# Stick-breaking attention: meta columns of four blocks turned in one transpose, first tokens' values added behind PSUM, 528 scores as 256 and 272

## The chip, the cores and the metric

The kernel runs on one core of a Trainium2 chip. The metric is the device time of one execution in microseconds, as the median of several runs. A core has five engines with a queue each, which run their instructions in order and wait for each other through semaphores: TensorE (PE in the profile; its weight loads are PEld), VectorE (DVE), ScalarE (ACT), GpSimd (POOL) and SyncE (SP), which issues the DMAs here. Tiles lie in SBUF; matmuls write to PSUM, which has eight banks of 128 x 512 float32.

## The reference

A decoder layer with two attention branches on the same normalized input: 16 meta tokens, then 2048 tokens, model width 1024. One branch is stick-breaking attention with 8 heads of 64:

```python
def stick_breaking_attention(q, k, v, valid):
    ...
    for blk in range(L // BLOCK):
        q0 = blk * BLOCK
        end = q0 + BLOCK
        z = jnp.einsum('bqhd,bkhd->bhqk', q[:, q0:end], k[:, :end],
                       preferred_element_type=jnp.float32) * scale
        ...
        mask = (s[None, :] < t[:, None]) & valid[None, :end]
        log_beta = jax.nn.log_sigmoid(z)
        log_1m = jnp.where(mask, log_beta - z, 0.0)
        rev = lax.cumsum(log_1m, axis=3, reverse=True)
        suffix = jnp.concatenate([rev[..., 1:], jnp.zeros_like(rev[..., :1])], axis=-1)
        w = jnp.where(mask, jnp.exp(log_beta + suffix), 0.0)
        outs.append(jnp.einsum('bhqk,bkhd->bqhd', w.astype(v.dtype), v[:, :end]))
    return jnp.concatenate(outs, axis=1)
```

The weight of a key is the product of `1 - sigmoid` over the keys between it and the query, times its own sigmoid. So with `r` the running product of `sigmoid(-z)` from the query backwards, the weights are differences of neighbours in `r`, and the sum over keys can be written as `r` times differences of neighbouring values, plus the value of the first token behind the query. The kernel computes it in that form. The other branch is a sliding-window attention with sinks; gates, two branch projections, an output projection and norms surround both.

## The kernel before

Tokens run in reverse order in four groups of 512 (`g`), in two halves: groups 2 and 3 first, then 1 and 0. Precision is kept by splitting each float32 operand into a high and a low part (`h`, `l`), so that most products are three matmuls. Each half has three stages. The first computes the projections for both branches and, woven between them, the sliding-window attention (`attend`). In the second, `stick` is woven into the gate projections (`tiles_by_tile`, `gemm`, L454) by `weave`, which hands out steps of `stick` by a credit that `cost_sb` sets. The third is other gate work (half 0) or the output (half 1).

The order of TensorE's instructions is written by hand over the whole kernel (`manual_schedule`); those of the other engines and the DMA queue are, for most stages, put in order by a scheduler. SP issues almost all DMAs.

`stick` runs over units: one head `h` (8) and one query group `g` (4), 32 units. In a unit, `row(h, g, n, j)` computes the scores of query block `j` (128 queries) against the next four key blocks: two matmuls per bank (L916), a sigmoid out of PSUM by ScalarE into `r` (L920), and a running product by DVE (`tensor_tensor_scan`, L928 or L930). The last row of a block (`end`) also has the 16 meta columns. For `j` = 0 it has 512 + 16 = 528 columns, more than a bank holds: `own` rows put the 16 into a second bank `zm` with two more matmuls (L918) and one more activation (L922). The others end with 400, 272 and 144 columns.

`turn`, `lt` steps later (6 in half 0, 5 in half 1), transposes blocks of rows with up to four transposes into a bank `t` (L941) and evicts them split into high and low (`evac_split`, L119 by ScalarE, L120 by DVE). At the end of a unit `turn_meta` transposes the meta columns of the four blocks, four transposes of 16 columns each into `zm` (L952), and evicts them split into rows 0 to 15 and 32 to 47 of `wm` (one of two 128x512 tiles).

`values` (L967) takes the turned tiles two steps later and accumulates weights times value differences in bank `o`, of which there is one. The unit's last matmul there takes `wm` against `vm[:, p, a]`, 128 rows: the meta differences in rows 0 to 15 and 32 to 47, and in rows from 64 the first tokens' values of the blocks, picked by constants in `wm` from row 64 on, which are set by a memset and an `affine_select` (L859, L860) at the start of each `stick`. Then `o` is copied out by ScalarE (L971) and stored. The next unit's first matmul into `o` waits for that copy.

`sb_v` in the projection stages makes the value differences. Its `firsts` (called by `late`) takes the first token's values of eight blocks, gathered in `vf`, transposes them (L578), splits them and writes them to `vm` by a DMA; there are eight such calls. `meta` makes the meta differences and `turned` puts them into `vm` (L594 and after), once for each of four pairs of heads, in half 0; L596 copies them to rows 32 to 47.

POOL does the splitting of weights in half 0's stick stage (L115, L116) and the causal masking of rows in half 1's (`affine_select`, L925).

Of the kernel before, what the change touches and what calls it, by code (L numbers as in the profile page):

```python
# [16 lines left out]
P = 128  # L17
# [31 lines left out]
def tile_kernel(ctx, tc, x, xt, meta, metat, gain, w_in, w_sb, w_sw, w_out, sinks, fgain,  # L49
# [23 lines left out]
    vn = cp.tile([P, 4], F32, name="vn")  # L73
    vf = cp.tile([P, 16], F32, name="vf")
    cp.tile([P, 40], F32, name="pad")
    ident = cp.tile([P, P], F32, name="ident")
# [11 lines left out]
    for i in range(IDLE):  # L88
        T.matmul(idle[:, :8 * 48], lhsT=mx.rearrange("p k t -> p (k t)")[:, :P], rhs=mx.rearrange("p k t -> p (k t)"), start=True, stop=True)
    V.memset(f32(vm), 0.0)  # L90

# [456 lines left out]
    def sb_v(p):  # L548

        def use(g, acc, ms):  # L550
            t, d = tmp(), tmp()
            A.copy(t, acc)
            V.tensor_tensor(d[:, :GT - 1], t[:, 1:], acc[:, :GT - 1], op=ALU.subtract)
            f0 = p % 2 * 8
            A.copy(vf[:, f0 + g % 2 * 4:f0 + g % 2 * 4 + 4], t.rearrange("p (b q) -> p b q", b=4)[:, :, 0])

# [17 lines left out]

            def firsts():

                tr = ps("zm")
                T.transpose(tr[:8, :P], vf[:, f0:f0 + 8], ident)  # L578
                vb = tmp(F32R)[:8, :2 * P].rearrange("p (a d) -> p a d", a=2)
                meta_rows(tr[:8, :P], vb[:, :, 0:64], vb[:, :, 64:128])  # L580
                DMA(vm[64 + 4 * g:72 + 4 * g, p], vb)

            def meta():
# [8 lines left out]
                def turned():  # L592
                    tr = ps("t")
                    T.transpose(tr[:NM, :P], md, ident)  # L594
                    meta_rows(tr[:NM, :P], vm[0:NM, p, :, 0:64], vm[0:NM, p, :, 64:128])
                    A.copy(vm[32:32 + NM, p], f32(vm[0:NM, p]))  # L596
                    rows()
                soon.append(turned)

            if ms is None:  # L600
                join(vn[:, p:p + 1] if g % 2 else vf[:, f0 + 4:f0 + 5])
            pending.append(rows if ms is None else meta)
            if g % 2 == 0:
                pending.append(lambda: late.append(firsts))
        return weights(C_SBV + p * P), use, "back"
# [242 lines left out]
    def stick(groups, bp):  # L848
# [4 lines left out]
        for tag, shape, n in (("q1", [P, GT], 2), ("q2", [P, GT], 2), ("v", [P, 4, P], 5), ("wh", [P, GT], 3), ("wl", [P, GT], 3),  # L853
                              ("k", [P, KW], 2)):
            for _ in range(n):
                bp.tile(shape, F32R, tag=tag, name=tag, bufs=n)
        for g in groups:
            w = wm[g % 2]
            G.memset(f32(w), 1.0)  # L859
            G.affine_select(out=w, in_=f32(w), pattern=[[-1, 4], [0, P]], compare_op=ALU.is_equal, fill=0.0,  # L860
                            base=-64 - 4 * g, channel_multiplier=1)
        av_todo = []
# [36 lines left out]
        def row(h, g, n, j):  # L899
# [10 lines left out]
            k0 = (b0 - 4 * groups[0]) * P  # L910
            own = end and nb == 4
            z = ps("z")
            zm = ps("zm") if own else None
            for t, qt in enumerate(st["q"]):
                lq = qt[:, j * P:(j + 1) * P]
                T.matmul(z[:, :w], lhsT=lq, rhs=kt[h][:, k0:k0 + w], start=t == 0, stop=t == 1)  # L916
# [3 lines left out]
            A.activation(r[:, :w], z[:, :w], AF.Sigmoid, scale=-1.0)  # L920
            if own:
                A.activation(r[:, w:w + NM], zm[:, :NM], AF.Sigmoid, scale=-1.0)  # L922
                w += NM
            if n == 0 and mask is None:
# [6 lines left out]
            last[j] = r[:, w - 1:w]  # L931
            rows_of[h, g, n, j] = r

        def turn(h, g, n, i):
# [13 lines left out]
        def turn_meta(h, g):  # L948
            p, a = divmod(h, 2)
            tr = ps("zm")  # L950
            for j in range(4):
                T.transpose(tr[:NM, j * P:(j + 1) * P], rows_of[h, g, 3 - g, j][:, GT - P * j:GT - P * j + NM], ident)  # L952
            w = wm[g % 2]
            evac_split(w[0:NM], w[32:32 + NM], tr[:NM])
            av_todo.append((h, g, vm[:, p, a, :], w, None, False, True))

        def values():
# [10 lines left out]
            if last:  # L968
                p, a = divmod(h, 2)
                u = tmp()  # L970
                A.copy(u, o)  # L971
                for n in range(2):
                    DMA(od[p][g][n][64 * a:64 * a + 64], u[64 * n:64 * n + 64])
# [5 lines left out]
        for s in range(n + lt + 3):  # L979
# [4 lines left out]
            if 0 <= t < n:  # L984
# [336 lines left out]
    for half, groups in enumerate(halves):  # L1321
# [61 lines left out]
        with tc.tile_pool(name=f"sb{half}", bufs=1, side="left") as bp:  # L1383
# [106 lines left out]
```

## Time and profile before

| | us |
|---|---|
| median of three runs | 2112.88 (2112.0 to 2113.49) |
| the profiled execution | 2112.16 |
| its span, first to last instruction | 2110.4 |
| stick-breaking of half 0 within it | about 374 to 592 |
| stick-breaking of half 1 within it | about 1092 to 1612 |

The profile is one execution. Busy time is given for each engine; matmuls are pipelined, so that the duration of one is longer than the distance to the next, and TensorE's cost of a piece of work is read from start to start. A row of a group reads: line, engine, operation, out<-in, partitions x elements, count | busy us, mean ns of one | idle time of the engine before them, and what ended it. A row of a timeline reads: start, length, engine, line, operation, tiles, count. A row of waits reads: who waited for whom, us in total, times, longest. What two matmuls in a row do in the same bank is merged into one row (x2).

### The profile page before, as it was taken

The numbers are of one execution on the slowest core, as the hardware profiler recorded it, in microseconds if no ns is written. First come the engines' busy times: TensorE is split into PE (matmuls) and PEld (weight loads), VectorE is DVE, ScalarE is ACT, GpSimd is POOL, SyncE is SP. The second block draws the span as 40 slices with busy tenths as digits, with TensorE's granted clock in tenths as the row PEclk, the third lists the DMA queues.
The fourth block names the chain that finished last, engine by engine and source line by source line (L and its number), as shares of the span: only waits on it lengthen the run. The fifth ranks groups of instructions, "written<-read, shape, count | busy, mean of one in ns | idle before, by whom it ended". The sixth has DMA issues, their size and how long they took to land.

```text
span 2110.4 us, 30845 instructions
## 1 busy us (share of the span) xinstructions
PE 2094.4 (99%) x10695; PEld 1755.2 (83%) x10695; DVE 1479.1 (70%) x2375; ACT 1058.8 (50%) x2438; POOL 300.1 (14%) x484
## 2 busy tenths in 40 slices
PE   9999999999999999999999999999999999999998
PEld 7888888888878888888888888888888888788887
DVE  7897986888878554887738888877774456564553
ACT  6677774555646335777735555555553202221131
POOL 2133444211000000232310000000000232000000
PEclk9999999999999999999999999999999999999999
DMA  9955545766449674435455344343424996568532
GB/s 337 324 174 193 191 168 181 238 194 200 139 142 338 232 256 155 152 136 178 137 172 153 123 126 127 118 125 95 123 88 142 360 323 203 181 232 309 160 100 90
DMA packets 169580, 391.07 MB, mean 185 GB/s; under 512 B 23601, under 2 KB 27697, under 8 KB 169425
## 3 DMA queue, kind: packets, MB, share of 16 engines
q1 hardware_dynamic: 169136, 388.84, 54.9%
q8 instruction: 85, 1.39, 0.3%
q14 instruction: 71, 0.57, 0.1%
q10 hardware_dynamic: 288, 0.27, 0.0%
HBM read 241.68 MB, written 145.18 MB: 183 GB/s over the span
## 4 chain that ended last, share of the span: by engine, by line
PE 91%; DVE 3%; ACT 3%; DMA 2%; issue 1%; SPq 0%; ACTq 0%; DVEq 0%
PE ps_g L454 39%; PE ps_o L967 6%; PE ps_z L916 6%; PE ps_t L941 6%; PE ps_z L754 3%; PE ps_o L810 2%; PE ps_g L252 1%; PE ps_g L253 1%; PE ps_g L251 1%; PE ps_z L252 1%; PE ps_z L251 1%; PE ps_z L253 1%; PE ps_t L252 1%; PE ps_t L253 1%; PE ps_t L251 1%; PE ps_t L788 1%
## 5 line engine op out<-in xcount | busy, mean ns | idle before, releaser
L454 PE MATMUL ps_g<-xh,wh 128*128 128x512 f32 x1296 | 532.1, 411 | 0.8 <-DVE tmp L675 0.5
L454 PE MATMUL ps_g<-xl,wh 128*128 128x512 f32 x1296 | 507.6, 392 | 0.4 <-DVE xl L1169 0.3
L454 PE MATMUL ps_g<-xh,wl 128*128 128x512 f32 x1296 | 507.7, 392 | 0.0
L930 DVE TENSOR_TENSOR_SCAN row<-row 128x512 f32<-128x512 f32 (+4 forms) x256 | 297.1, 1161 | 91.9 <-ACT row L920 39.5
L454 PEld LDWEIGHTS ps_g<-xh,wl 128*128 128x128 f32 x1296 | 243.3, 188 | 54.4 <-DVE wl L1217 0.4
L920 ACT ACTIVATE row<-ps_z 128x512 f32<-128x512 f32 (+1 forms) x320 | 172.4, 539 | 213.5 <-PE ps_z L916 192.3
L454 PEld LDWEIGHTS ps_g<-xh,wh 128*128 128x128 f32 x1296 | 244.3, 188 | 41.4 <-ACT xh L1168 1.0
L454 PEld LDWEIGHTS ps_g<-xl,wh 128*128 128x128 f32 x1296 | 244.8, 189 | 37.8 <-DVE xl L1169 1.7
L119 ACT ACTIVATE wth<-ps_t 128x512 fp32r<-128x512 f32 (+1 forms) x320 | 170.7, 533 | 76.3 <-PE ps_t L941 75.2
L120 DVE SCALAR_TENSOR_TENSOR wtl<-ps_t,wth 128x512 fp32r<-128x512 f32 (+1 forms) x320 | 188.9, 590 | 25.3 <-ACT wth L119 24.8
L916 PE MATMUL ps_z<-kt,q 128*128 128x512 f32 (+3 forms) x640 | 185.3, 369 | 0.0
L941 PE MATMUL ps_t<-ident,row 128*128 128x128 f32 x1088 | 171.7, 273 | 0.1
L941 PEld LDWEIGHTS ps_t<-ident,row 128*128 128x128 f32 x1088 | 134.7, 140 | 34.0 <-DVE wtl L120 1.3
L916 PEld LDWEIGHTS ps_z<-kt,q 128*128 128x128 f32 x640 | 117.9, 188 | 23.5
L967 PE MATMUL ps_o<-wth,vc 128*128 128x512 f32 (+1 forms) x320 | 130.2, 407 | 0.0
L967 PE MATMUL ps_o<-wtl,vc 128*128 128x512 f32 (+1 forms) x320 | 116.3, 363 | 0.0
L762 ACT ACTIVATE sc<-sc,nm 128x129 f32<-128x129 f32 x256 | 100.0, 393 | 27.9 <-DVE nm L760 26.9
L115 POOL TENSOR_SCALAR wh<-raw 128x1024 fp32r<-128x1024 f32 (+1 forms) x47 | 52.8, 1124 | 354.0 <-PE ps_g L454 143.4
L610 ACT ACTIVATE tmp<-ps_g 128x512 f32<-128x512 f32 x84 | 50.3, 598 | 74.1 <-PE ps_g L454 67.0
L925 POOL TENSOR_SCALAR_AFFINE_SELECT row<-row 128x128 f32<-128x128 f32 x64 | 20.4, 318 | 468.2 <-ACT row L920 441.0
L290 ACT CAST ringl<-gt 128x512 fp32r<-128x512 f32 x32 | 19.9, 622 | 129.0 <-DVE gt L288 127.1
L794 POOL TENSOR_SCALAR_AFFINE_SELECT pm<-pl 64x256 fp32r<-64x256 f32 x128 | 74.3, 580 | 37.3 <-DVE pl L120 31.9
(441 smaller groups left out, 4130.1 us busy)
## 6 DMA issues: line engine op xcount, KB each, us to landing
wh<-h_in_w_in SPq DMA_DIRECT2D x66, 512.0 KB, 3.7
wl<-l_in_w_in SPq DMA_DIRECT2D x66, 512.0 KB, 4.9
h_in_w_in<-wh SPq DMA_DIRECT2D x50, 512.0 KB, 3.3
l_in_w_in<-wl SPq DMA_DIRECT2D x50, 512.0 KB, 3.5
raw<-in_w_in SPq DMA_DIRECT2D x49, 512.0 KB, 5.3
q<-qd SPq DMA_DIRECT2D x128, 128.0 KB, 3.3
vc<-vd SPq DMA_DIRECT2D x48, 256.0 KB, 3.1
kd<-tmp SPq DMA_DIRECT2D x32, 256.0 KB, 3.3
```

The costliest lines, as they stand in the source:

```text
L119: A.activation(h, acc, AF.Copy, scale=scale)
L120: V.scalar_tensor_tensor(l, acc, scale, f32(h), op0=ALU.mult, op1=ALU.subtract)
L251: T.matmul(acc, lhsT=wh[:, k, :], rhs=h, start=k == 0, stop=False)
L252: T.matmul(acc, lhsT=wh[:, k, :], rhs=l, start=False, stop=False)
L454: T.matmul(acc, lhsT=a[:, k, :], rhs=b[:, k, :], start=k == i == 0, stop=k == KT - 1 and i == 2)
L762: A.activation(sc[:, hh, :], sc[:, hh, :], AF.Exp, bias=nm[:, hh:hh + 1], accum_out=den[:, hh:hh + 1])
L794: G.affine_select(out=pm[to, :, c], in_=full[r, :, c], pattern=[[0, 4], [sign, HB]], compare_op=ALU.is_ge, fill=0.0, base=n - 1, channel_m ...
L916: T.matmul(z[:, :w], lhsT=lq, rhs=kt[h][:, k0:k0 + w], start=t == 0, stop=t == 1)
L920: A.activation(r[:, :w], z[:, :w], AF.Sigmoid, scale=-1.0)
L930: V.tensor_tensor_scan(r[:, :w], r[:, :w], r[:, :w], last[j] if n else 1.0, op0=ALU.mult, op1=ALU.min)
L941: T.transpose(tr[:, j * P:(j + 1) * P], rows_of[h, g, n - (j > i), j][:, k0:k0 + P], ident)
L967: T.matmul(o[:, :n], lhsT=v, rhs=r, start=first and r is wh, stop=last)
```

## The change

- `turn_meta`: the 16 meta columns of an end row are copied by POOL into a tile `m` of the unit, split into high and low (two operations for each end row, four end rows a unit). One transpose turns the 128 columns of `m` (4 blocks x 2 parts x 16) at once; four copies, two by ScalarE and two by DVE, put the 32 rows of each block beside its own 128 columns of `wm`, which is zero elsewhere (block-diagonal). The `wm` are set to zero once at the start, and their constants go.
- `vm` holds the meta differences in all 128 rows, eight times; three DMAs from SBUF to SBUF double them, each from what the one before wrote.
- First tokens: `firsts` goes. `vf` keeps the first values by column; POOL copies them into `vfirst`, which has a head's values in its half of the partitions and zeros in the other. `values` adds them as it evicts `o`: four activations of 128 columns with a bias for each partition, in place of one copy of 512.
- Own rows: 528 scores are 256 in a bank `z` and 272 in `zm`, two matmuls and one sigmoid each.
- The step costs handed to `weave` for `turn_meta` become 0.11 for 0.43, and `cost_sb` follows. `dynamic_dma_scratch_size=1024` and a wider `pad` move what lies where in SBUF.

```diff
-    vf = cp.tile([P, 16], F32, name="vf")
-    cp.tile([P, 40], F32, name="pad")
+    vf = cp.tile([P, 4, 8], F32, name="vf")
+    vfirst = [cp.tile([P, 4, 8], F32, name=f"vf{a}") for a in range(2)]
+    cp.tile([P, 88], F32, name="pad")
...
-    V.memset(f32(vm), 0.0)
+    for t in (*(f32(w) for w in wm), *vfirst):
+        G.memset(t, 0.0)
...
-            def firsts():
-
-                tr = ps("zm")
-                T.transpose(tr[:8, :P], vf[:, f0:f0 + 8], ident)
-                vb = tmp(F32R)[:8, :2 * P].rearrange("p (a d) -> p a d", a=2)
-                meta_rows(tr[:8, :P], vb[:, :, 0:64], vb[:, :, 64:128])
-                DMA(vm[64 + 4 * g:72 + 4 * g, p], vb)
...
-                    A.copy(vm[32:32 + NM, p], f32(vm[0:NM, p]))
+                    for n in (NM, 2 * NM, 4 * NM):
+                        DMA(vm[n:2 * n, p], vm[0:n, p])
...
             if g % 2 == 0:
-                pending.append(lambda: late.append(firsts))
+                for a, t in enumerate(vfirst):
+                    r = slice(64 * a, 64 * a + 64)
+                    G.tensor_copy(t[r, p], vf[r, p])
...
-        for g in groups:
-            w = wm[g % 2]
-            G.memset(f32(w), 1.0)
-            G.affine_select(out=w, in_=f32(w), pattern=[[-1, 4], [0, P]], compare_op=ALU.is_equal, fill=0.0,
-                            base=-64 - 4 * g, channel_multiplier=1)
...
-            own = end and nb == 4
-            z = ps("z")
-            zm = ps("zm") if own else None
+            pieces = [("z", 0, w)]
+            if end and nb == 4:
+                pieces = [("z", 0, w // 2), ("zm", w // 2, w // 2 + NM)]
+                w += NM
+            banks = [ps(tag) for tag, _, _ in pieces]
             for t, qt in enumerate(st["q"]):
-                lq = qt[:, j * P:(j + 1) * P]
-                T.matmul(z[:, :w], lhsT=lq, rhs=kt[h][:, k0:k0 + w], start=t == 0, stop=t == 1)
-                if own:
-                    T.matmul(zm[:, :NM], lhsT=lq, rhs=kt[h][:, k0 + w:k0 + w + NM], start=t == 0, stop=t == 1)
+                for z, (_, c, m) in zip(banks, pieces):
+                    T.matmul(z[:, :m], lhsT=qt[:, j * P:(j + 1) * P], rhs=kt[h][:, k0 + c:k0 + c + m], start=t == 0, stop=t == 1)
             r = bp.tile([P, RW], F32, tag="row", name="row", bufs=12)
-            A.activation(r[:, :w], z[:, :w], AF.Sigmoid, scale=-1.0)
-            if own:
-                A.activation(r[:, w:w + NM], zm[:, :NM], AF.Sigmoid, scale=-1.0)
-                w += NM
+            for z, (_, c, m) in zip(banks, pieces):
+                A.activation(r[:, c:c + m], z[:, :m], AF.Sigmoid, scale=-1.0)
...
+            if end:
+                if j == 0:
+                    st["m"] = bp.tile([P, 4, 2, NM], F32R, tag="m", name="m", bufs=2)
+                mh, ml = (st["m"][:, j, i, :] for i in range(2))
+                mr = r[:, w - NM:w]
+                G.tensor_scalar(mh, mr, 1.0, 1.0, op0=ALU.mult, op1=ALU.mult)
+                G.tensor_tensor(ml, mr, f32(mh), op=ALU.subtract)
...
             tr = ps("zm")
+            T.transpose(tr[:, :P], f32(state[h, g]["m"]).rearrange("p j i k -> p (j i k)"), ident)
+            w = wm[g % 2]
             for j in range(4):
-                T.transpose(tr[:NM, j * P:(j + 1) * P], rows_of[h, g, 3 - g, j][:, GT - P * j:GT - P * j + NM], ident)
-            w = wm[g % 2]
-            evac_split(w[0:NM], w[32:32 + NM], tr[:NM])
+                r = slice(32 * j, 32 * j + 32)
+                (V.tensor_copy if j % 2 else A.copy)(w[r, j * P:(j + 1) * P], tr[r, :P])
...
-                A.copy(u, o)
+                for j in range(4):
+                    c = slice(j * P, (j + 1) * P)
+                    A.activation(u[:, c], o[:, c], AF.Identity, bias=vfirst[a][:, p, g % 2 * 4 + j:g % 2 * 4 + j + 1])
...
-                    yield 0.43
+                    yield 0.11
...
-            cost_sb = 8 * sum(4 * (4 - g) for g in groups) * 1.31 + 16 * 0.75 + LT[half] * 0.86
+            cost_sb = 8 * sum(4 * (4 - g) for g in groups) * 1.31 + 16 * 0.33 + LT[half] * 0.86
...
-    nc = bacc.Bacc("TRN2", target_bir_lowering=False, num_devices=1)
+    nc = bacc.Bacc("TRN2", target_bir_lowering=False, num_devices=1, dynamic_dma_scratch_size=1024)
```

More of the change, by code (lines that the diff above doesn't have):

```diff
@@ L553, in use @@
             V.tensor_tensor(d[:, :GT - 1], t[:, 1:], acc[:, :GT - 1], op=ALU.subtract)
-            f0 = p % 2 * 8
-            A.copy(vf[:, f0 + g % 2 * 4:f0 + g % 2 * 4 + 4], t.rearrange("p (b q) -> p b q", b=4)[:, :, 0])
+            A.copy(vf[:, p, g % 2 * 4:g % 2 * 4 + 4], t.rearrange("p (b q) -> p b q", b=4)[:, :, 0])
             def join(nxt):
@@ L600, in use @@
             if ms is None:
-                join(vn[:, p:p + 1] if g % 2 else vf[:, f0 + 4:f0 + 5])
+                join(vn[:, p:p + 1] if g % 2 else vf[:, p, 4:5])
             pending.append(rows if ms is None else meta)
             if g % 2 == 0:
-                pending.append(lambda: late.append(firsts))
+                for a, t in enumerate(vfirst):
+                    r = slice(64 * a, 64 * a + 64)
+                    G.tensor_copy(t[r, p], vf[r, p])
         return weights(C_SBV + p * P), use, "back"
@@ L853, in stick @@
         for tag, shape, n in (("q1", [P, GT], 2), ("q2", [P, GT], 2), ("v", [P, 4, P], 5), ("wh", [P, GT], 3), ("wl", [P, GT], 3),
-                              ("k", [P, KW], 2)):
+                              ("k", [P, KW], 2), ("m", [P, 4, 2, NM], 2)):
             for _ in range(n):
                 bp.tile(shape, F32R, tag=tag, name=tag, bufs=n)
-        for g in groups:
-            w = wm[g % 2]
-            G.memset(f32(w), 1.0)
-            G.affine_select(out=w, in_=f32(w), pattern=[[-1, 4], [0, P]], compare_op=ALU.is_equal, fill=0.0,
-                            base=-64 - 4 * g, channel_multiplier=1)
         av_todo = []
```

## The prediction

> **What bounds the kernel now.** First the page: its span, its first part, and the shares by engine in the chain that ended last.
>
> ```profile
> span 2110.4 us, 30845 instructions
> PE 2094.4 (99%) x10695; PEld 1755.2 (83%) x10695; DVE 1479.1 (70%) x2375; ACT 1058.8 (50%) x2438; POOL 300.1 (14%) x484
> PE 91%; DVE 3%; ACT 3%; DMA 2%; issue 1%; SPq 0%; ACTq 0%; DVEq 0%
> ```
>
> TensorE is busy for all but 16 us, and the chain lies on it for 91%. But matmuls are pipelined in this profile, so a busy share hides small stalls, and I asked for the busy time of the two stretches that the change touches most (stick-breaking of half 0, then of half 1), and for the waits in the first.
>
> ```profile
> 376.00:592.00 216.00, 215.91 (x1213) 182.35 (x1213) 175.50 (x231) 120.06 (x258) 27.19 (x17) 1.00 0.59 183
> 1092.00:1612.00 520.00, 519.95 (x2804) 435.04 (x2804) 400.68 (x484) 276.43 (x537) 20.37 (x64) 1.00 0.40 120
> PEld ps_t L941 <- DVE wtl L120: 0.7, 2, 0.4
> PEld ps_o L967 <- ACT tmp L971: 0.2, 1, 0.2
> ```
>
> The columns of the first two rows are length, then busy time of PE, weight load, DVE, ACT, POOL. TensorE has no gap at a granted clock of 1.00; DVE has 19% and 23% free, ACT 44% and 47%. Only two waits reach TensorE's weight loads, below 1 us together. So TensorE's instruction stream is the time here: what is taken out of it comes off one for one, and what makes it wait adds one for one. TensorE's order is written by hand, so both can be counted. Prices must be starts against starts, not durations.
>
> **The change, part by part.** *Meta transposes, 4 to 1 for each head and group.*
>
> ```profile
> 386.18 0.38 PE L941 MATMUL ps_t<-ident,row 128*128 128x128 f32 x2
> 386.32 0.47 PE L967 MATMUL ps_o<-wth,vc 128*128 128x512 f32 x1
> 386.63 0.39 PE L967 MATMUL ps_o<-wtl,vc 128*128 128x512 f32 x1
> ...
> 387.92 0.27 PE L941 MATMUL ps_t<-ident,row 128*128 128x128 f32 x1
> 388.03 0.60 PE L952 MATMUL ps_zm<-ident,row 128*16 128x128 f32 x4
> 388.38 0.48 PE L454 MATMUL ps_g<-xh,wh 128*128 128x512 f32 x1
> 388.70 0.39 PE L454 MATMUL ps_g<-xl,wh 128*128 128x512 f32 x1
> 388.93 0.39 PE L454 MATMUL ps_g<-xh,wl 128*128 128x512 f32 x1
> L952 PE MATMUL ps_zm<-ident,row 128*16 128x128 f32 x128 | 19.2, 272 | 0.0
> L578 PE MATMUL ps_zm<-ident,vf x8: 270/271/275, 104.2 to 1057.4; 128*8 128x128 f32 x8
> ```
>
> Two wide matmuls in a row start 0.32 us apart right after transposes (388.38 to 388.70), so a run of transposes also delays the matmul behind it. I take a run from its first start to the second start behind it, less 0.23 us, the ordinary distance of two 512-column matmuls (388.70 to 388.93). Two transposes: 386.18 to 386.63 less 0.23 is 0.22. Five (one plus four of L952): 387.92 to 388.70 less 0.23 is 0.55. Three transposes are worth 0.33 us. There are 128/4 = 32 such runs: 32 x 0.33 = 10.6 us. The new transpose has 128 weight columns, as L941 has, which cost the same 0.11 each.
>
> *First tokens.* The eight transposes of L578 go, with their evictions and DMAs: 8 x 0.11 = 0.9 us. The others' work was beside TensorE.
>
> *Own rows, 512+16 becoming 256+272.*
>
> ```profile
> 374.46 0.39 PE L916 MATMUL ps_z<-kt,q 128*128 128x512 f32 x1
> ...
> 375.37 0.39 PE L454 MATMUL ps_g<-xl,wh 128*128 128x512 f32 x1
> ...
> 376.89 0.41 PE L916 MATMUL ps_z<-kt,q 128*128 128x272 f32 x2
> 377.13 0.40 PE L454 MATMUL ps_g<-xh,wh 128*128 128x512 f32 x1
> 377.37 0.40 PE L454 MATMUL ps_g<-xl,wh 128*128 128x512 f32 x1
> ```
>
> Same reckoning: an own row now takes 374.46 to 375.37 less 0.23, 0.68 us; the 16-column matmuls are too short for the weight load behind them. A pair of 272 columns takes 376.89 to 377.37 less 0.23, 0.25 us, and 0.24 without what it leaves behind. Two pairs of about that width: 0.49 us. Saved 0.19 for one row of each head and group, 32: 6.1 us. **Taken out in all: 10.6 + 0.9 + 6.1 = 17.6 us.**
>
> *The wait that is added.* Bank o is single. Its eviction at a unit's end was one copy of 512 columns; it is four activations of 128 columns with a bias read per partition. The next unit's first value matmul waits for it, and behind that in TensorE's queue stands everything else. ScalarE's prices, and one such boundary in half 1 (the timeline of 1244.9 to 1246.9 us):
>
> ```profile
> L971 ACT COPY tmp<-ps_o 128x512 f32<-128x512 f32 x32 | 18.8, 587 | 20.0 <-PE ps_o L967 18.2 <-DMA q<-qd 0.7 <-DMA raw<-in_w_in 0.7
> L119 ACT ACTIVATE wth<-ps_t 128x128 fp32r<-128x128 f32 x32 | 8.8, 275 | 2.9 <-PE ps_t L941 2.9
> L424 ACT CAST xh<-xs 128x512 fp32r<-128x512 f32 x22 | 13.6, 621 | 15.2 <-DVE xs L423 14.7
> L1168 ACT ACTIVATE uh<-raw,gn 128x512 fp32r<-128x512 f32 x4 | 2.6, 710 | 0.0
> 1245.12 0.39 PE L967 MATMUL ps_o<-wm,vm 128*128 128x512 f32 x1
> 1245.55 0.59 ACT L971 COPY tmp<-ps_o 128x512 f32<-128x512 f32 x1 [0.74 <-PE ps_o L967]
> 1246.04 0.60 ACT L920 ACTIVATE row<-ps_z 128x512 f32<-128x512 f32 x1
> 1246.63 0.48 PE L967 MATMUL ps_o<-wth,vc 128*128 128x512 f32 x1
> 579.17 0.58 ACT L971 COPY tmp<-ps_o 128x512 f32<-128x512 f32 x1
> 579.80 0.19 PEld L967 LDWEIGHTS ps_o<-wth,vc 128*128 128x128 f32 x1 [0.22 <-ACT tmp L971]
> ```
>
> The new form isn't in the trace. A 128-column eviction from PSUM takes 0.275 us. An operand read per partition (gn) makes 0.621 into 0.710, so 0.09 more: 0.364. Back to back, ScalarE starts the next 0.49 us into a 0.59 us one, an overlap of 0.10. Four: 4 x 0.364 - 3 x 0.10 = 1.16 us, where the copy took 0.59. Bounds: 4 x 0.275 - 0.3 = 0.80 if the bias cost nothing, 4 x 0.364 = 1.46 with no overlap. I take 1.16, since each piece of it has a row.
>
> In the boundary shown the eviction starts 0.43 us after the meta matmul and the next value matmul 1.51 us after it. By 579.17 + 0.58 to 579.80 a freed bank reaches the weight load in 0.05 us; with the load's own lead I take 0.08. The new eviction frees the bank at 0.43 + 1.16 + 0.08 = 1.67. In half 0 an own row lies in that window and shrinks it: 0.23 (meta matmul) + 0.49 + 3 x 0.23 + 0.14 (two transposes, 386.18 to 386.32) = 1.55. The changed kernel's TensorE order has 30 boundaries: 16 with two transposes last (9 in half 1 of 1.51 us, wait 0.16; 7 in half 0 of 1.55, wait 0.12; 2.3 us); 9 with wide matmuls last, some 0.1 longer (0.1 each with the late weight load, 0.9); 4 with six wide matmuls, no wait; and one at the end of half 0's stick, with nothing but two transposes between (0.23 + 0.14, wait 1.3). At three of them another eviction stands right ahead on ScalarE, for which I add 1 us together. **Wait: 2.3 + 0.9 + 1.3 + 1 = 5.5 us**; by the bounds, about 1 us at 0.80, and 0.3 more on 26 boundaries at 1.46, 13 us.
>
> The Trainium skill, ScalarE: Activation LUTs, "What ACT_TABLE_LOAD costs", gives 280 ns + 0.833 ns a column for an activation whose bias is a per-partition operand, with 93 ns of overlap. By it the four would take 4 x 387 - 3 x 93 = 1.27 us and the time would be 3 us above mine, an estimate by that page; the 275 ns row, which reads PSUM, lies below the page's sum and I keep it.
>
> *What is covered.* POOL gets two 16-column operations for each end row, 256 in all, needed only five or six steps (of over 2 us) later, when the one transpose comes. DVE loses one 16x512 eviction for each unit and gains two copies of 32x128. SP gets three DMAs in a chain, each waiting for the one before, four times in half 0's window stage; SP is in order, so weight loads, vd stores and xs copies stand behind them.
>
> ```profile
> kd<-tmp SPq DMA_DIRECT2D x8, 8.0 KB, 1.5
> 96.43 0.45 SPq L59 DMA_DIRECT2D raw<-in_w_in  x1
> 106.42 1.56 POOL L115 TENSOR_SCALAR wh<-raw 128x1024 fp32r<-128x1024 f32 x1 [5.53 <-DMA l_in_w_in<-wl]
> ```
>
> A DMA of this size lands in 1.5 us. The weight load issued at 96.43 now stands behind the first of the chain and two stores; it is used at 106.42, ten microseconds later. I cost it at nothing; without that cover it would be some 3 us of four chains, up to 12 us once.
>
> **Sum.** 2112.16 (this execution's time, 1.8 us around its span) - 17.6 + 5.5 = 2100.1. The median of the three runs is 0.7 above that execution, so 2101 in round numbers.
>
> **The rivals.** *No wait at bank o* (the window is long enough): 2112.9 - 17.6 + 0.8 for the last boundary = 2096. For it: 0.16 us is little against the reading of one boundary. Against: every piece has a row and ScalarE was free at 1245.55.
>
> *Bank o waits much longer*: if the four don't overlap, 13 us, and 14 with a sigmoid eviction ahead of them once or twice: 2112.9 - 17.6 + 14 = 2109. ScalarE's free 44% speaks against queueing.
>
> *The split does not do what it says*: each of the four score matmuls bound by its weight load.
>
> ```profile
> L916 PEld LDWEIGHTS ps_z<-kt,q x640: 187/188/192, 374.2 to 1599.5; 128*128 128x128 f32 x160
> ```
>
> 4 x 0.188 = 0.75 instead of 0.49, so 32 x 0.26 = 8.3 us are lost again: 2109. The pair of 272 at 0.24 speaks against it.
>
> *Slower: DVE becomes the bound in half 0's stick*, through POOL's new operations.
>
> ```profile
> 387.26 1.30 DVE L930 TENSOR_TENSOR_SCAN row<-row 128x528 f32<-128x528 f32 x1
> 394.43 2.39 POOL L116 TENSOR_TENSOR wl<-raw,wh 128x1024 fp32r<-128x1024 f32 x1
> 395.16 2.78 DVE L928 TENSOR_TENSOR_SCAN row<-row,mask 128x528 f32<-128x528 f32 x1 [0.36 <-ACT row L922]
> L747 POOL COPY sc<-skb 128x4 f32<-128x4 f32 x64 | 19.5, 311 | 407.5 <-PE ps_t L788 221.1 <-PE ps_g L1099 158.4 <-DMA skb<-in_sinks 14.4
> ```
>
> A scan that takes 1.30 us alone took 2.78 beside a POOL operation of 2.39. DVE is busy 175.5 of 216 us there, and TensorE would leave it about 208. 128 of the new POOL operations fall into that stretch, so DVE has 33 us, 0.26 for each, before it decides. At 0.45 each it adds 128 x 0.45 - 33 = 25 us: 2126. By the nearest row a POOL operation that small takes 0.31 us, and at 1.48/2.39 of that (0.19) DVE keeps 9 us. The Trainium skill, GPSIMD Engine Reference, "8. Key points", says that POOL shares its SBUF interfaces with VectorE and contends with instructions of two SBUF inputs; the 2.78 us agrees.
>
> **How the numbers follow.** Forecast (2101, its own range 2098 to 2106) 0.60; no wait (2096) 0.17; long wait (2109) 0.10; split without gain (2109) 0.06; DVE the bound (2126) 0.07. The range 2095 to 2110 takes in both bounds of the eviction and leaves out the slower case and edges. A change within 0.2% (4.2 us) can't be told from none here: faster is below 2108.7. The first two and 0.03 of the long wait give faster 0.80; the rest of the two cases at 2109 gives same 0.13; slower 0.07.
>
> **What would show it.** A run of the one new transpose with the one before it 0.33 us shorter; own rows at 0.49 us; the four evictions 1.16 us from first start to last end; weight loads of L967's first value matmul idle on ScalarE some 0.1 to 0.2 us at most boundaries, and once above 1 us near 580 us. It is wrong if TensorE waits for POOL's m or for DVE's wtl in the stick stretches by more than 2 us, if weight loads wait on DMAs between 95 and 340 us, or if the time is above 2110.

## The result, and the profile after

| | before | after |
|---|---|---|
| median of 8 runs each, taken together, us | 2111.85 (2110.71 to 2114.31) | 2106.07 (2103.94 to 2107.41) |
| ratio, 95% interval | | 0.9969 (0.996 to 0.9979) |
| profiled execution, us | 2112.16 | 2105.11 |
| its span, us | 2110.4 | 2103.4 |

The change makes the kernel 5.8 us faster (7.0 us between the two profiled executions). The forecast was 2101, in a range from 2095 to 2110: right sign, inside the wide range, at the edge of the forecast's own range (2098 to 2106), and half the gain that the sum gave (5.8 us for 11.9).

First the same views as before. The page's head and first part, of the changed kernel (line numbers are the new ones: scores L909, sigmoids L912, scans L917 and L919, m L927 and L928, transposes L937, the meta transpose L947, wm copies L951, values L964, the biased evictions L970, the gate matmuls L456, `evac_split` L121 and L122, weight splitting by POOL L117 and L118):

```profile
span 2103.4 us, 31216 instructions
PE 2080.9 (99%) x10591; PEld 1744.2 (83%) x10591; DVE 1482.2 (70%) x2398; ACT 1066.8 (51%) x2554; POOL 372.6 (18%) x752
```

TensorE's busy time fell by 13.5 us, the span only by 7.0: TensorE now stands idle for 22.5 us where it was 16.0. The busy times of the first stick stretch (length, then PE, weight load, DVE, ACT, POOL) and its waits show where:

```profile
376.00:592.00 216.00, 212.50 (x1176) 179.13 (x1175) 177.73 (x250) 125.35 (x324) 65.44 (x141) 1.00 0.59 183
```

```profile
ACT wm L951 <- DVE wm L951: 15.5, 12, 4.0
...
PEld ps_o L964 <- ACT tmp L970: 3.1, 7, 1.3
...
PEld ps_o L964 <- DVE wm L951: 1.4, 2, 1.2
...
PE ps_t L937 <- DVE wtl L122: 1.3, 2, 1.2
...
PE ps_o L964 <- DMA zs<-tmp: 1.1, 1, 1.1
...
PE ps_o L964 <- ACT tmp L970: 1.0, 1, 1.0
```

The first stretch now has 3.5 us without a matmul where it had 0.1. Three of these waits were not in the forecast's sum: TensorE's for `wtl` (the low part of the turned rows, which DVE evicts), TensorE's for DVE's part of `wm` (the row that names a DMA is that matmul too, below), and, first of all, ScalarE's 15.5 us of waiting for DVE's part of `wm`.

For the accounts I cut each trace at TensorE's own landmarks: the starts of the first score matmul and of the last meta matmul of each half. What lies between them is called the stick of that half. "Counted" is what the prediction takes out, 17.7 us by stage; it allows for three gate matmuls more in each stick (0.7 us), which the new credits of `weave` move there from the stage behind.

| us | before | after | counted | measured |
|---|---|---|---|---|
| start | 374.46 | 373.90 | -0.5 | -0.6 |
| stick of half 0 | 215.05 | 213.30 | -7.7 | -1.8 |
| gates and first stage of half 1 | 522.03 | 522.31 | -1.1 | +0.3 |
| stick of half 1 | 499.77 | 494.65 | -7.7 | -5.1 |
| rest | 499.06 | 499.22 | -0.7 | +0.2 |
| sum | 2110.36 | 2103.39 | -17.7 | -7.0 |

So 10.7 us of the counted gain are lost in this execution, where the forecast set 5.5 us against it.

What was counted is there. The timeline of TensorE at one meta transpose and, further on, at one unit's end in half 1, with ScalarE:

```profile
387.74 0.27 PE L937 MATMUL ps_t<-ident,row 128*128 128x128 f32 x1
387.85 0.27 PE L947 MATMUL ps_zm<-ident,m 128*128 128x128 f32 x1
387.88 0.42 PE L964 MATMUL ps_o<-wth,vc 128*128 128x384 f32 x1
388.13 0.34 PE L964 MATMUL ps_o<-wtl,vc 128*128 128x384 f32 x1
388.31 0.39 PE L456 MATMUL ps_g<-xh,wh 128*128 128x512 f32 x1
...
1242.48 0.40 PE L964 MATMUL ps_o<-wm,vm 128*128 128x512 f32 x1
1242.91 1.14 ACT L970 ACTIVATE tmp<-ps_o,vf 128x128 f32<-128x128 f32 x4 [0.84 <-PE ps_o L964]
...
1244.11 0.50 PE L964 MATMUL ps_o<-wth,vc 128*128 128x512 f32 x1
1244.45 0.39 PE L964 MATMUL ps_o<-wtl,vc 128*128 128x512 f32 x1
1244.68 0.28 PE L909 MATMUL ps_z<-kt,q 128*128 128x256 f32 x1
...
1245.16 0.40 PE L456 MATMUL ps_g<-xh,wh 128*128 128x512 f32 x1
1245.40 0.39 PE L456 MATMUL ps_g<-xl,wh 128*128 128x512 f32 x1
```

The run with the meta transpose takes 387.74 to 388.13, less the 0.18 us from there to the next start: 0.21, where it was 0.55. The other runs agree: reckoned in this way, a run costs 0.11 us for each transpose, from one alone (in the changed kernel) to eight (before, 0.87), so that 96 fewer are the 10.6 us. The own row takes 1244.68 to 1245.40 less 0.23, 0.49 as forecast. The four evictions take 1.14 us (forecast 1.16), and the next value matmul stands 1244.11 - 1242.48 = 1.63 us behind the meta matmul (forecast 1.67, before 1.51). The Trainium skill, ScalarE: Activation LUTs, "What ACT_TABLE_LOAD costs", gives an estimate of 1.27 us for the four; the trace has 1.14 here, so the page's sum is too high for this source in PSUM. For the same operation on SBUF (e5, below) the trace has 1.28, and there it fits.

The groups of the new operations (line, engine, operation, count | busy us, mean ns | idle before, and for whom):

```profile
L928 POOL TENSOR_TENSOR m<-row,m 128x16 fp32r<-128x16 f32 x128 | 45.4, 355 | 10.0
...
L970 ACT ACTIVATE tmp<-ps_o,vf 128x128 f32<-128x128 f32 x128 | 36.6, 371 | 18.7 <-PE ps_o L964 18.1 <-DMA gs<-tmp 0.2
...
L951 DVE CAST wm<-ps_zm 32x128 fp32r<-32x128 f32 x64 | 18.6, 290 | 5.8 <-ACT wm L951 4.2
L951 ACT CAST wm<-ps_zm 32x128 fp32r<-32x128 f32 x64 | 16.1, 252 | 24.2 <-DVE wm L951 21.0 <-PE ps_zm L947 1.4
```

A biased eviction of 128 columns is 371 ns (forecast 364). The copies of `wm` are short, but ScalarE idles 21.0 us before its own, waiting for DVE's. The four copies of a unit go to four disjoint blocks of `wm`, yet in the trace they run one after the other, ACT, DVE, ACT, DVE; what orders them no run shows. Two places in half 0 show what that does:

```profile
442.01 2.39 POOL L118 TENSOR_TENSOR wl<-raw,wh 128x1024 fp32r<-128x1024 f32 x1
442.15 2.83 DVE L919 TENSOR_TENSOR_SCAN row<-row 128x272 f32<-128x272 f32 x1
...
445.01 0.30 DVE L951 CAST wm<-ps_zm 32x128 fp32r<-32x128 f32 x1
...
445.36 0.19 PEld L964 LDWEIGHTS ps_o<-wm,vm 128*128 128x128 f32 x1 [1.20 <-DVE wm L951]
445.37 0.50 PE L964 MATMUL ps_o<-wm,vm 128*128 128x512 f32 x1 [1.06 <-DMA zs<-tmp]
...
467.46 2.39 POOL L118 TENSOR_TENSOR wl<-raw,wh 128x1024 fp32r<-128x1024 f32 x1
...
468.05 2.66 DVE L919 TENSOR_TENSOR_SCAN row<-row 128x400 f32<-128x400 f32 x1
...
470.62 0.26 DVE L122 SCALAR_TENSOR_TENSOR wtl<-ps_t,wth 128x128 fp32r<-128x128 f32 x1
470.91 0.28 DVE L951 CAST wm<-ps_zm 32x128 fp32r<-32x128 f32 x1
470.94 0.55 PE L937 MATMUL ps_t<-ident,row 128*128 128x128 f32 x3 [1.17 <-DVE wtl L122]
471.23 0.26 ACT L951 CAST wm<-ps_zm 32x128 fp32r<-32x128 f32 x1 [4.00 <-DVE wm L951]
```

At 442 a scan beside POOL's splitting takes 2.83 us; DVE's last copy into `wm` stands behind it, and the meta matmul, which the hand-written order puts there, waits 1.1 us for that copy. At 468 another such scan holds DVE's `wtl` (a wait of 1.17 us on TensorE) and DVE's first copy, and ScalarE stands still for 4.0 us, with sigmoids and evictions behind it.

### The profile page after: what moved, and what is told of

Same layout as the page of the kernel before. It is cut to its first block, busy times and chain, and to the rows that moved or that the text cites. A ratio compares the mean times of both kernels' runs of the same rounds, so it can differ in the third digit from the quotient of the medians.

```text
span 2103.4 us, 31216 instructions
## 1 busy us (share of the span) xinstructions
PE 2080.9 (99%) x10591; PEld 1744.2 (83%) x10591; DVE 1482.2 (70%) x2398; ACT 1066.8 (51%) x2554; POOL 372.6 (18%) x752
## 5 line engine op out<-in xcount | busy, mean ns | idle before, releaser
L456 PE MATMUL ps_g<-xh,wh 128*128 128x512 f32 x1296 | 529.6, 409 | 2.8 <-issue 1.1
L456 PE MATMUL ps_g<-xl,wh 128*128 128x512 f32 x1296 | 507.7, 392 | 0.7 <-DVE xl L1168 0.6
L456 PE MATMUL ps_g<-xh,wl 128*128 128x512 f32 x1296 | 507.3, 391 | 0.1
L919 DVE TENSOR_TENSOR_SCAN row<-row 128x512 f32<-128x512 f32 (+4 forms) x256 | 296.2, 1158 | 82.4 <-ACT row L912 42.9
L456 PEld LDWEIGHTS ps_g<-xh,wl 128*128 128x128 f32 x1296 | 243.3, 188 | 54.3 <-DVE wl L118 0.6
L456 PEld LDWEIGHTS ps_g<-xh,wh 128*128 128x128 f32 x1296 | 244.1, 188 | 42.1 <-ACT xh L1167 1.5
L456 PEld LDWEIGHTS ps_g<-xl,wh 128*128 128x128 f32 x1296 | 244.7, 189 | 38.9 <-DVE xl L1168 2.0
L912 ACT ACTIVATE row<-ps_z 128x512 f32<-128x512 f32 (+2 forms) x320 | 166.0, 519 | 183.1 <-PE ps_z L909 178.2
L122 DVE SCALAR_TENSOR_TENSOR wtl<-ps_t,wth 128x512 fp32r<-128x512 f32 (+1 forms) x320 | 189.7, 593 | 25.2 <-ACT wth L121 23.5
L121 ACT ACTIVATE wth<-ps_t 128x512 fp32r<-128x512 f32 (+1 forms) x320 | 171.5, 536 | 64.8 <-PE ps_t L937 62.5
L909 PE MATMUL ps_z<-kt,q 128*128 128x512 f32 (+4 forms) x640 | 178.7, 354 | 0.0
L937 PE MATMUL ps_t<-ident,row 128*128 128x128 f32 x1088 | 171.2, 272 | 1.9 <-DVE wtl L122 1.9
L937 PEld LDWEIGHTS ps_t<-ident,row 128*128 128x128 f32 x1088 | 134.9, 140 | 34.5 <-DVE wtl L122 2.9
L909 PEld LDWEIGHTS ps_z<-kt,q 128*128 128x128 f32 x640 | 117.5, 188 | 21.9
L964 PE MATMUL ps_o<-wth,vc 128*128 128x512 f32 (+1 forms) x320 | 132.0, 413 | 1.1 <-ACT tmp L970 1.0
L964 PE MATMUL ps_o<-wtl,vc 128*128 128x512 f32 (+1 forms) x320 | 116.2, 363 | 0.0
L927 POOL TENSOR_SCALAR m<-row 128x16 fp32r<-128x16 f32 x128 | 29.2, 228 | 415.4 <-DVE row L919 387.9
L117 POOL TENSOR_SCALAR wh<-raw 128x1024 fp32r<-128x1024 f32 (+1 forms) x47 | 52.2, 1110 | 234.2 <-PE ps_g L456 96.5
L790 POOL TENSOR_SCALAR_AFFINE_SELECT pm<-ph 64x256 fp32r<-64x256 f32 x128 | 62.2, 486 | 108.9 <-ACT ph L121 104.7
```

Of the source, the lines that this page charges most:

```text
L121: A.activation(h, acc, AF.Copy, scale=scale)
L122: V.scalar_tensor_tensor(l, acc, scale, f32(h), op0=ALU.mult, op1=ALU.subtract)
L456: T.matmul(acc, lhsT=a[:, k, :], rhs=b[:, k, :], start=k == i == 0, stop=k == KT - 1 and i == 2)
L909: T.matmul(z[:, :m], lhsT=qt[:, j * P:(j + 1) * P], rhs=kt[h][:, k0 + c:k0 + c + m], start=t == 0, stop=t == 1)
L912: A.activation(r[:, c:c + m], z[:, :m], AF.Sigmoid, scale=-1.0)
L919: V.tensor_tensor_scan(r[:, :w], r[:, :w], r[:, :w], last[j] if n else 1.0, op0=ALU.mult, op1=ALU.min)
```

## The experiments

All are variants of one of the two kernels; each ratio is to the kernel before, measured beside it (medians 2111.9 to 2113.3). Theory: the missing gain is the wait for bank o plus the waits that DVE's lateness makes, in the places above; the rivals were a price of POOL's new operations, and prices of the matmuls that were counted wrongly. All variants of the changed kernel keep its order of TensorE's instructions, which the new credits of `weave` make another than before, so no run tests what that order alone does.

**e1, o evicted by one copy.** The first tokens' values are left out of the result here.

```diff
-                for j in range(4):
-                    c = slice(j * P, (j + 1) * P)
-                    A.activation(u[:, c], o[:, c], AF.Identity, bias=vfirst[a][:, p, g % 2 * 4 + j:g % 2 * 4 + j + 1])
+                A.copy(u, o)
```

> Leaves out the first tokens' values: bank o is evicted by one copy of 512 columns again; all else as changed. Theory of bank o (the four evictions take 1.15 us and hold TensorE at 26 of 30 boundaries for 0.15 to 0.2 us, and 1 us once): about 5 us below the changed kernel, near 2101, and the next value matmul 1.5 to 1.6 us behind the meta matmul instead of 1.63. Rival (the eviction is hidden, the missing gain lies elsewhere): within 1 us of 2106.

Measured: 2100.46, ratio to before 0.9944 (0.9931 to 0.9956), so 5.6 us below the changed kernel's 2106.07. The 30 windows from a meta matmul to the second value matmul behind it shrink from 62.07 to 58.06 us, so 4.0 us are the bank itself; the sticks together are 3.2 us shorter. The other stages take the same in the two traces (1395.4 and 1395.6 us), and the two profiled executions differ by 3.1 us; what makes the medians differ by 2.4 us more is not in the traces. The waits that don't belong to bank o stay (whole run):

```profile
ACT wm L951 <- DVE wm L951: 21.4, 21, 4.0
...
PE ps_t L937 <- DVE wtl L122: 2.2, 4, 1.2
...
PE ps_o L964 <- DVE wm L951: 1.2, 1, 1.2
...
PE ps_o L964 <- ACT tmp L968: 0.5, 1, 0.5
```

The third row is the wait that the changed kernel's trace had put down to a DMA: the same matmul, here at 444.95 us, now named for what it is. The last is the end of half 0's stick, where only two transposes cover: 1.0 us with the four evictions, 0.5 with the copy.

**e2, all four wm copies by ScalarE.**

```diff
-                (V.tensor_copy if j % 2 else A.copy)(w[r, j * P:(j + 1) * P], tr[r, :P])
+                A.copy(w[r, j * P:(j + 1) * P], tr[r, :P])
```

> All four copies of the turned meta columns by ScalarE, none by DVE; result unchanged. Theory of the alternating copies (ScalarE stands up to 4 us behind DVE's copy, which stands behind scans; 15.5 us of such waits in half 0's stick, and two waits of TensorE of 1.1 us each follow from it): 2 to 3 us below the changed kernel, near 2103.5, no wait of ScalarE's wm copies for DVE. Rival (ScalarE's waits are covered; DVE is late because of POOL alone): the same as the changed kernel within 1 us, the two waits of TensorE near 444 and 469 us stay.

Measured: 2103.93, 0.996 (0.9947 to 0.9972), 2.1 below the changed kernel. Half 0's stick takes 211.42 instead of 213.30, half 1's the same 494.65. ScalarE's wait for `wm` is gone, and so is the stop at 444; the stop of TensorE for `wtl` is not (first stretch):

```profile
PEld ps_o L964 <- ACT tmp L970: 2.9, 6, 1.3
...
PE ps_t L937 <- DVE wtl L122: 1.2, 1, 1.2
```

**e3, own rows as 512 and 16 again**, the rest of the change kept.

```diff
-                pieces = [("z", 0, w // 2), ("zm", w // 2, w // 2 + NM)]
+                pieces = [("z", 0, w), ("zm", w, NM)]
```

> Own rows as 512 and 16 again, all else as changed. Theory: 32 own rows take 0.19 us more each, 6.1 us; in half 0 the own row lies in the window of bank o, whose wait shrinks by about 0.15 at 12 boundaries, 1.8 us: 4 to 5 us above the changed kernel, near 2110.5. Rival (the split gains nothing in the end): 2106.

Measured: 2108.8, 0.9984 (0.9975 to 0.9993): 2.7 us above the changed kernel (3.6 in the sticks), less than expected.

**e4, e1 and e2 together.**

> The first two together (first tokens' values left out, one copy out of bank o, wm copies all by ScalarE). If both losses are real and add: 7 to 8 us below the changed kernel, near 2098.5, and what is left against the count of 17.6 us is 4 us that lie elsewhere. If only bank o counts: 2101. If neither: 2106.

Measured: 2100.55, 0.9944 (0.993 to 0.9958). Its sticks take 210.25 and 493.05 us, 4.6 below the changed kernel, which is nearly the sum of e1's 3.2 and e2's 1.9. But the median is e1's, and 2 us above the 2098.5 expected. Stages that no edit touches differ by a few us between kernels (below), so the medians of single edits can't be added to better than that; the sticks nearly can.

**e8, the own rows alone**: the kernel before, with nothing but 256 and 272 in its own rows.

> The kernel before with the own rows alone as 256 and 272. Counted gain: 32 x 0.19 = 6.1 us, near 2106.4, if nothing else moves. Rival (a part of each gain is lost to later waits on DVE or ScalarE, since DVE is 81% busy in half 0's stick): 2108 or above, with new waits of TensorE on wtl.

Measured: 2108.19, 0.9977 (0.9968 to 0.9986), 5.2 us faster where 6.1 were counted, and no new wait of a matmul in the sticks. The order of TensorE's instructions is the same in both, so each own row can be compared from its first start to the second start behind it. Where a wide matmul stands behind it, the row saves 0.19 us, as the prediction read; where transposes stand behind, 0.14 to 0.15 (one of them, at 1123 us, saves nothing, since the transpose behind it waits for `wtl` in both kernels); over the 32 rows, 16 of each kind, 5.3 us. One with transposes behind, before:

```profile
473.75 0.39 PE L916 MATMUL ps_z<-kt,q 128*128 128x512 f32 x1
...
474.32 0.17 PE L918 MATMUL ps_zm<-kt,q 128*128 128x16 f32 x1
474.35 0.42 PE L941 MATMUL ps_t<-ident,row 128*128 128x128 f32 x2
474.52 0.48 PE L967 MATMUL ps_o<-wth,vc 128*128 128x512 f32 x1
474.84 0.39 PE L967 MATMUL ps_o<-wtl,vc 128*128 128x512 f32 x1
```

and the same row in e8:

```profile
472.23 0.28 PE L918 MATMUL ps_z<-kt,q 128*128 128x256 f32 x1
...
472.71 0.38 PE L939 MATMUL ps_t<-ident,row 128*128 128x128 f32 x2
472.85 0.48 PE L965 MATMUL ps_o<-wth,vc 128*128 128x512 f32 x1
473.16 0.39 PE L965 MATMUL ps_o<-wtl,vc 128*128 128x512 f32 x1
```

1.09 us become 0.93: 0.16. In the row of the prediction a wide matmul stood behind. Over the same 32 rows e3 differs from the changed kernel by 5.3 us at the second start behind the own row but by 3.9 at the seventh, for at most boundaries of half 0 the own row lies in the window of bank o, and some 0.1 us of what it saves is waited for there. That accounts for 1.4 us of what e3 missed.

**e12, the own rows as 512 and 16 in e5** (e5 is below; it has neither the wait for bank o nor the one for `wm`).

> e5 with its own rows as 512+16 again. The counted price of that is 32 x 0.195 = 6.2 us; put into the changed kernel it cost only 2.7 us (e3), alone in the kernel before it gained 5.2 (e8). Theory that in the changed kernel the waits for bank o and for the wm copies took up part of it, because a longer own row gives them time: without these waits the own rows cost the counted sum, and this takes 2105 to 2106.5, half 0's stick 212.2 to 212.8 and half 1's 495.6 to 496.2. Rival, that the split gains less than counted wherever the meta transposes are gone (its shorter rows bring ScalarE's second sigmoid and DVE's scan late): 2102 to 2104.

Measured: 2103.55, 0.9956 (0.9943 to 0.997), 3.9 above e5's first median and 2.9 above its second; the sticks are 2.1 and 2.6 us longer, 4.7 together. The first theory's number fails. But the rival's mechanism isn't it either: row by row the same pattern appears as in e8, 0.19 or 0.14 to 0.15 by what follows. Over the 32 rows 5.1 us are left here at the seventh start behind, against 3.9 in e3, so the waits did take up a part, as the first theory has it; but the price was counted too high from the start, in either kernel.

**e7, POOL's m operations moved**: e2, with the high part by ScalarE and the low part by DVE.

```diff
-                G.tensor_scalar(mh, mr, 1.0, 1.0, op0=ALU.mult, op1=ALU.mult)
-                G.tensor_tensor(ml, mr, f32(mh), op=ALU.subtract)
+                A.copy(mh, mr)
+                V.tensor_tensor(ml, mr, f32(mh), op=ALU.subtract)
```

> As the kernel with wm copies all by ScalarE (2103.9), and m's two operations by ScalarE and DVE in place of POOL. Theory that POOL's new operations make DVE late: the wait of TensorE on DVE's wtl near 468 us goes and the time falls by 1 to 2 us, to 2102 to 2103. Rival (that wait comes from POOL's splitting of weights, L117 and L118, whose place among the steps has shifted): it stays, and the time is 2104 or a little more, since DVE has 64 more small operations in each stretch.

Measured: 2107.16, 0.9977 (0.9968 to 0.9985), 3.2 slower than e2. The profiled execution is the slowest of its eleven (2112.22), so its trace shows where the waits lie and not how long a usual one is. In the first stretch the wait for `wtl` stays (0.9 us, at 477), and TensorE waits for bank o 4.2 us in place of 1.0. ScalarE now stands 40.2 us in 53 waits for DVE's scans before it copies `m`: once more it inherits DVE's queue. So on ScalarE and DVE these operations cost more. That POOL's are not what makes DVE late isn't shown by this run alone, since it gives DVE work in their place; e11, below, keeps them, and there the wait goes.

**e5 and e6, the four evictions replaced.** `o` is copied out at once, so that the bank comes free as before, and the first values are added in SBUF: in e5 by four activations of ScalarE, in e6 by one operation of POOL; the `wm` copies as in e2.

```diff
+                A.copy(u, o)
                 for j in range(4):
                     c = slice(j * P, (j + 1) * P)
-                    A.activation(u[:, c], o[:, c], AF.Identity, bias=vfirst[a][:, p, g % 2 * 4 + j:g % 2 * 4 + j + 1])
+                    A.activation(u[:, c], u[:, c], AF.Identity, bias=vfirst[a][:, p, g % 2 * 4 + j:g % 2 * 4 + j + 1])
```

> Bank o is evicted by one copy of 512 columns, and the first tokens' values are added behind it, in SBUF, by four activations of ScalarE; wm copies all by ScalarE. Result complete. If only the time at which bank o comes free counts, as the kernel without first tokens' values showed (2100.5): 2100 to 2101.5. Rival (ScalarE's added 1.3 us a unit delays its next evictions and TensorE with them): 2103 to 2106.

> As the one before, but the first tokens' values are added by one POOL operation of 128x512 a unit. Bank o as freed by the copy: 2100.5. Rival (POOL beside DVE: a two-input operation of 1.3 us stretches a scan by some 0.8 us, 32 times, where DVE is 80% busy): 2102 to 2105, with more waits of TensorE on DVE's wtl.

Measured: e5 2099.67, 0.9937 (0.9925 to 0.995); e6 2100.43, 0.9939 (0.9926 to 0.9953). Both beat both kernels. Sticks: 209.54 and 492.96 in e5, 210.00 and 493.07 in e6. In the first stretch one stop of TensorE for `wtl` is left, near 468 us, 0.7 us in e5 and 1.2 in e6.

**e9, e10 and e11, what makes DVE late near 467.** e9 is e5 with half 0's weight splitting taken from POOL; e10 is e5 once more beside it; e11 is e6 with e9's edit.

```diff
-            hsplit[0] = vsplit[0] = False
+            hsplit[0] = vsplit[0] = half == 0
```

> The kernel of e5 (o copied out, first values added by ScalarE, wm copies by ScalarE), with the weight splitting of half 0's stick-breaking stage given to ScalarE (high part) and VectorE (low part) in place of POOL. In e5 a wait of 0.7 us is left near 467 us, where a transpose waits for DVE's wtl copy behind a scan of 2.20 us that runs beside POOL's 3.21 us splitting (128x400, 1.05 us when alone). Theory that POOL's splitting makes DVE late there: the stretched scans (over 2 us) go in 376 to 592 us, the transposes' waits for wtl with them, half 0's stick takes 208.0 to 209.0 us instead of 209.5, and the time is 0.5 to 1.5 us below e5: 2098.2 to 2099.2. Rival, that DVE is late because of its own work: seven splittings of 1.22 us are added to it, 8.5 us, the waits for wtl stay or grow, and the time is e5's or up to 3 us above (2099.7 to 2103).

> The kernel of e5 once more, beside e9 on one chip: 2099.7, between 2098.5 and 2101, if e5's first measurement holds; it is the figure that e9 is to be compared with.

Measured: e9 2099.59, 0.9938 (0.9925 to 0.9952); e10 2100.67, 0.9944 (0.9932 to 0.9957). The two are not told apart. The wait goes from 0.7 to 0.5 only, and half 0's stick from 209.57 to 209.35, where 209.0 or less was expected. DVE did get faster, though: in the first stretch, the group of the 400-column scans in e10 and then in e9,

```profile
L919 DVE TENSOR_TENSOR_SCAN row<-row 128x400 f32<-128x400 f32 x8 | 10.4, 1298 | 0.5 <-ACT row L912 0.5
```

```profile
L919 DVE TENSOR_TENSOR_SCAN row<-row 128x400 f32<-128x400 f32 x8 | 8.4, 1045 | 0.5 <-ACT row L912 0.5
```

and no scan is over 1.32 us. What was left in e9 was another cause, seen in its timeline: the four activations in SBUF, 1.28 us together, stand ahead of an own row's two sigmoids on ScalarE, and DVE stands idle for 1.97 us before the row's scan.

```profile
462.60 1.28 ACT L971 ACTIVATE tmp<-tmp,vf 128x128 f32<-128x128 f32 x4
463.78 0.36 ACT L912 ACTIVATE row<-ps_z 128x256 f32<-128x256 f32 x1
464.05 0.38 ACT L912 ACTIVATE row<-ps_zm 128x272 f32<-128x272 f32 x1
...
464.53 1.32 DVE L919 TENSOR_TENSOR_SCAN row<-row 128x528 f32<-128x528 f32 x1 [1.97 <-ACT row L912]
```

e6 hasn't got these, but has the stretched scans. e11 takes both away:

> e6 (o copied out, first values added by one POOL operation, wm copies by ScalarE) with e9's splitting of half 0's weights by ScalarE and VectorE. e6 and e9 each keep one of two causes for a late DVE near 467 us: e6 the scans stretched by POOL's splitting (its wait for wtl is 1.2 us), e9 four activations of 1.28 us ahead of an own row's sigmoids on ScalarE, so that the row's scan starts 1.97 us late (its wait is 0.5 us). Theory that these two are the causes: with both gone the transposes wait below 0.3 us for wtl there, half 0's stick takes 208.4 to 209.2 us (209.35 in e9, 210.0 in e6), and the time is 0.3 to 1.3 us below e9, some 2098.8. Rival, that something else keeps DVE late: a wait of 0.5 us or more stays near 467 us and the time is e9's or above, 2099.6 to 2101.

Measured: half 0's stick 208.62 us, as expected, and no transpose waits for `wtl` in the first stretch any more; its only waits on TensorE's two queues are

```profile
PEld ps_o L964 <- ACT tmp L968: 1.6, 3, 0.7
...
PE ps_o L964 <- ACT tmp L968: 0.7, 2, 0.5
```

So the two causes are shown for that place: with either of them left (e6, e9) a wait stays, with both gone there is none. The time, 2100.49 with 0.9939 (0.9926 to 0.9951), is not below e9's, against the expectation: the stages outside the sticks take 1397.3 us in this profile, 1395.5 in e9's and 1393.1 in e5's. That spread is as large as anything left to win in the sticks.

## Why the prediction was half right

**What is taken out.** The meta transposes are as counted, 0.11 us each and so 0.33 less for each of the 32 units. The own rows were mis-sized: 5.2 us (e8) in place of 6.1, because the price was read off one row with a wide matmul behind it and used for all 32; half of them have transposes behind, and save 0.14 to 0.16, or in one case nothing. Nothing speaks against the 0.9 us of the first tokens' transposes, but they are too few to be seen.

**The wait at bank o.** Right in mechanism and nearly in size. Eviction 1.14 us for 1.16, bank free 1.63 for 1.67, the one long wait at the end of half 0 1.01 for 1.3; in all 4.0 us by the windows (e1) for 5.5. For keeping its eviction price below the page's the prediction set the page's sum against a 275 ns row that has no bias; the two are not of a kind, but the 0.364 us that it then used came out at 0.371.

**What is covered.** This step failed. "DVE loses one 16x512 eviction for each unit and gains two copies of 32x128" was weighed by length, and by length it is a gain. What was missed is that the copies alternate between two engines and run one after the other: ScalarE, which had 44% free, came to stand behind DVE's queue, 21.0 us in 21 waits, and TensorE's meta matmul behind DVE at 444. e2, which takes this away, and with it DVE's 64 short copies (18.6 us in all), gains 1.9 us in half 0's stick; a run with all four on DVE, which would tell the turns from DVE's load, was not made. Later in that stick DVE's lateness reaches a transpose (1.2 us near 469 in the changed kernel, gone in e11). A further wait for `wtl`, 0.58 us at 1120 us, is in the changed kernel and in every variant of it, and wasn't tried. The prediction had named waits for `wtl` of more than 2 us in the sticks as a sign of being wrong: they come to 2.9 us by TensorE's weight loads and 1.9 by its matmuls.

**POOL and the DMA chain.** Here the cover held. No run shows POOL's operations holding TensorE up (e11 keeps them, and half 0's stick is the shortest of all there); they take 228 and 355 ns on average where the nearest row had 311; the start, in which the chains of DMAs lie, is 0.6 us shorter where 0.5 was counted, and between 95 and 340 us no weight load waits for a DMA.

**The account.** In the two sticks 15.4 us were counted out and 6.9 came: 8.5 lost. Bank o 4.0, `wm` 1.9, `wtl` at 469 and 1120 1.8, own rows 0.9: 8.6. These come from different runs and partly overlap, so that the fit to 0.1 is luck; that nothing large is missing is not: e11, which has neither the four evictions at bank o nor the stops for `wm` and at 469, has sticks 13.1 us shorter than before, where 14.5 are counted with the own rows at their measured price. The other 2.2 us are outside the sticks: counted -2.3, measured -0.1. One stop of 1.1 us at 747 us is part of it, which is not in the kernel before nor in e1, e4, e5 or e6. Over all kernels these three stages together take 1393.1 to 1398.9 us, with nearly the same instructions; what sets that is open. That the time lies inside the range is in part luck: the range was made wide by the bounds of the eviction, the eviction came out close to its forecast, and waits that the sum put at nothing took up the room.

**The rivals.** "No wait at bank o" is refuted (1.63 us and not 1.51), and so are the long wait (the four overlap) and the split without gain (0.49 us). DVE as the bound is refuted as it was put: DVE is busy 177.7 of 216 us and not above TensorE. But that rival was nearest to what went wrong: DVE needn't be full to hold TensorE up, only late once behind a scan of 2.7 us, with an engine behind it that works in order.

## What to carry to other kernels

When work of one tile is dealt to two engines, ask who waits for whom between the pieces, not only how long they are: a free engine that takes its turn behind a busy one inherits that one's queue. Where, as here, matmuls wait for a single PSUM bank to come free, a tile is better moved out by one short copy, with the arithmetic behind it, in SBUF, on an engine with room (e5 and e6, which also have e2's copies: 2099.7 to 2100.7, about what was forecast for the change). And a price that depends on what stands next in a pipeline is read at each kind of neighbour, and each is counted.

## What was not expected of the hardware

What 16-column matmuls cost depends on what stands behind them: 256 and 272 columns in place of 512 and 16 saved 0.19 us ahead of a wide matmul and 0.14 to 0.16 ahead of transposes.

Taking seven splittings of a 128x1024 weight from POOL and giving their subtraction to DVE (1.22 us each, against 2.39 and more on POOL) made DVE less busy, not more: 168.9 us of the first stretch in e10, 165.6 in e9. The subtractions added 8.5 us, but half 0's 96 scans took 95.8 us in place of 105.4; most of the rest of the fall is one other instruction, 2.9 us long, which runs into that stretch in e10 alone. The Trainium skill, GPSIMD Engine Reference, "8. Key points", has POOL contend with VectorE instructions of two SBUF inputs for the interfaces to SBUF; the traces agree (a scan reads two), and give the amount: a scan of 1.05 us takes 2.66 beside a POOL operation of 2.39.
